# A decoder layer's second FFN: operands on 256-byte lines, weight sums on VectorE, two of eight pairs with seven products

## The chip, the cores and the metric

The kernel runs on one core of one Trainium2 chip. The metric is the device time of one execution in microseconds. A profile is taken of one further execution. In the profile PE is TensorE (its weight loads are listed as PEld), DVE is VectorE, ACT is ScalarE, POOL is GpSimd, and SP is the engine whose queue issues the weight loads from HBM.

## The reference, cut to what matters

One layer of a decoder, for 256 tokens and 16 meta tokens, width 2048, in float32. The change lies in the last step, the second SwiGLU FFN; the first FFN and the attention, convolution and merge ahead of it ("the mix") keep their instructions.

```python
D_MODEL, SEQ, D_FF = 2048, 256, 5632

def swiglu(x, w_gate, w_up, w_down):
    return (jax.nn.silu(x @ w_gate) * (x @ w_up)) @ w_down

h = h + 0.5 * swiglu(rms_norm(h, ffn1_norm_g), ffn1_w_gate, ffn1_w_up, ffn1_w_down)
...
u = rms_norm(h, ffn2_norm_g[l])
h = h + 0.5 * swiglu(u, ffn2_w_gate[l], ffn2_w_up[l], ffn2_w_down[l])
return h[:, N_META:]
```

## The kernel before, in words

**Numbers.** Every float32 operand is split into a high part (`whi`, rounded to the matmul's format) and a low part (`wlo`, what is left). A product of two such operands is three matmuls: high by high, high by low, low by high (`mac3`, lines 1053 to 1055).

**The weight stream.** Class `Stream` brings the weights in the order in which TensorE uses them. A load is 1 MB (128 rows of 2048 floats, tile `raw`), issued on SP's queue (line 130). It is cut into sub-blocks of at most 1024 columns. For each sub-block ScalarE writes `whi` (line 175) and VectorE writes `wlo = raw - whi` (line 176). `next()` hands the next block of weights to TensorE. When a new sub-block begins it first runs what was put off with `early`, then splits the sub-block that lies a fixed number of places ahead, then runs what was put off with `later`. So the program order of ScalarE and VectorE is set by these three calls. In the second FFN there are six pairs of buffers for split sub-blocks, and a sub-block is split five places ahead of TensorE: the split of sub-block n waits until TensorE has read sub-block n - 6.

**The second FFN.** The 5632 hidden columns are 11 groups of 512. An "up" group forms gate and up for all 256 tokens, from 8 pairs of 256 input rows. For each pair the work is a 2 x 2 by 2 x 2 block product (two halves of the tokens and of the input rows, against gate and up weights). A pair of kind `C` takes the eight plain products: 24 matmuls of 512 columns, two sub-blocks of 1024 columns. A pair of kind `S` takes seven products (the Strassen-Winograd form): 21 matmuls, from four sub-blocks: the weight sums `sa` (1024 columns) and `sb` (1024), two raw blocks (1024) and one (512). The sums of the weights are made by GpSimd (`sum` and `sum_rest`, lines 145, 159 and 160), the sums of the tokens by GpSimd as well (`sums_of_tokens`), once for each pair. The products are gathered in the eight PSUM banks `q1` to `q8`; the seven-product terms are put together on VectorE and ScalarE in `after_seven`, `after_gate`, `after_up` and `products`. Four of the eight pairs of every up group are `S`. A "down" step multiplies the gated result (`mid`, transposed by `turn_mid`) of two or three groups by the down weights, in two halves of 1024 output columns, all of it by plain products, and adds to `ht` (line 1215). `PLAN` lists the order: up, up, down and so on, one group behind.

**The start of the second FFN.** `act2` is the input in split form. The first group also transposes `h` into `ht` (`turn_h`, line 1110, after its first two pairs, into the banks `q1`, `q5`, `q6`, `q7`), makes two of the four token sums, and runs `norm2` (lines 1096 and 1100), which gives the scale `r2` that the gate needs.

**Places in SBUF.** Tiles stand in pools one behind the other, and unused `fill` tiles shift what follows. Counted from the sizes of the tiles, the streamed weight tiles of the pool `splitp` begin 192 bytes behind a multiple of 256 bytes, those of `split2` 224 bytes behind, `mid` of the second FFN 224, `more` (token sums) 192, and `act` on a multiple of 256. In the second FFN the weights are the moving operand of the matmul (512 columns) and the tokens the stationary one (128 columns); in the first FFN and most of the mix it is the other way round.

Of the kernel before, what the change touches and what calls it, by code (L numbers as in the profile page):

```python
# [76 lines left out]
class Stream:  # L77
# [7 lines left out]
    def __init__(self, nc, raw_pool, split_pool):  # L85
# [6 lines left out]
        self.seven, self.n_sums = [], 0  # L92
# [31 lines left out]
    def load(self, upto):  # L124
# [8 lines left out]
        self.sum()  # L133

    def sum(self):

        nc = self.nc
        while self.sum_pool and self.n_sums < len(self.seven):
            g = self.seven[self.n_sums]
            if g >= self.n_loaded or len(self.sums) > 1:  # L140
                return
            raw = self.raw[g]
            a21 = raw[:, 3 * WIDE :].rearrange("p (q c) -> p q c", q=1).to_broadcast([P, 2, WIDE])
            sa = self.sum_pool.tile([P, 2 * WIDE], F32, name="sa", bufs=2)
            nc.gpsimd.tensor_add(  # L145
                sa.rearrange("p (q c) -> p q c", q=2),
                raw[:, WIDE : 3 * WIDE].rearrange("p (q c) -> p q c", q=2),
                a21,
            )
            self.sums[g] = [sa, None]  # L150
            self.n_sums += 1
            if len(self.sums) == 1:
                self.sum_rest(g)

    def sum_rest(self, g):

        nc, raw, sa = self.nc, self.raw[g], self.sums[g][0]
        sb = self.sum_pool.tile([P, 2 * WIDE], F32, name="sb", bufs=1)
        nc.gpsimd.tensor_add(sb[:, :WIDE], sa[:, WIDE:], raw[:, WIDE : 2 * WIDE])
        nc.gpsimd.tensor_add(sb[:, WIDE:], sb[:, :WIDE], raw[:, :WIDE])  # L160
        self.sums[g][1] = sb

    def split(self, upto):
        nc = self.nc
        while self.n_split < min(upto, len(self.subs)):
            g, kind, c, kk, width = self.subs[self.n_split]
            self.load(g + self.raw_bufs)
            n = kk * width
            raw = self.raw[g] if kind == "raw" else self.sums[g][kind == "sb"]
            raw = raw[:, c : c + n]  # L170
# [4 lines left out]
            nc.scalar.activation(hi[:, :n], raw, AF.Copy)  # L175
            nc.vector.tensor_sub(lo[:, :n], raw, hi[:, :n].bitcast(F32))  # L176
# [4 lines left out]
            if kind == "sb":  # L181
                del self.sums[g]
                for x in self.sums:
                    self.sum_rest(x)
                self.sum()
# [48 lines left out]
def tile_decoder_layer(  # L234
# [56 lines left out]
    for kind, at in PLAN:  # L291
        for k, _ in pairs_of(at) if kind == "up" else [("C", 0)] * (len(at) * 4):
            st.add_pair(w2[i], k)
            i += 1
# [13 lines left out]
    const.tile([P, 56], F32, name="fill")  # L308
# [236 lines left out]
    with ExitStack() as mix:  # L545
# [4 lines left out]
        R2 = mp.tile([P, T], F32, name="R2")  # L550
# [458 lines left out]

        def sums_of_tokens(i, to, room):  # L1010
# [6 lines left out]
            nc.gpsimd.tensor_sub(t[:, 0, :], x[:, 0, :P], x[:, 0, P:])  # L1017
            nc.gpsimd.tensor_sub(t[:, 1, :], x[:, 0, P:], x[:, 1, P:])
            nc.gpsimd.tensor_add(t[:, 2, :], x[:, 1, P:], t[:, 0, :])
            nc.gpsimd.tensor_sub(t[:, 3, :], x[:, 1, :P], t[:, 2, :])  # L1020
# [5 lines left out]
        for d in range(KD):  # L1026
# [4 lines left out]
            if d in (1, 5):  # L1031
                st.later(lambda d=d: sums_of_tokens(d // 2, spare[:, d // 4], lambda x: soft_tile(x)[:, :WIDE]), 3)
# [11 lines left out]
    r2 = left.tile([P, 2 * NT], F32, name="r2")  # L1044
# [27 lines left out]
    mids, waiting = {}, []  # L1072

    def turn_mid(tags):
# [4 lines left out]
        pool = left if g % 3 == 2 else right[0]  # L1079
        to = pool.tile([P, 4, 2, SEQ], F32R, name="mid", tag=f"mid{g % 3}")  # L1080
        mids[g] = to
        for j in range(NT):
# [4 lines left out]
            def after(j=j, ps=ps):  # L1087
                cols = slice(j * P, (j + 1) * P)
                src = ps.rearrange("p (f t) -> p f t", f=4)
                split_into(to[:, :, 0, cols], to[:, :, 1, cols], src)  # L1090

            st.later(after, 1 + j)

# [19 lines left out]
    def up_group(g):  # L1113
        todo = pairs_of(g)
        kinds = [k for k, _ in todo]
# [246 lines left out]
```

## Time and profile before

| | us |
|---|---|
| median of three runs (2247.4 to 2256.06) | 2249.43 |
| the profiled execution | 2250.48 |
| its span, first to last instruction | 2248.7 |
| second FFN in it, from the last `po` product to the end | about 1450 to 2249 |
| PE busy over the span | 2180.6 |

How to read it: the profiled execution took 1.8 us more than its span and 1.05 us more than the median. A matmul's record ends after the next one has begun, so the time that a run of matmuls takes is read from their starts, not from the mean duration.

### The profile page before, as it was taken

The page shows a single profiled execution, that of the slowest core. Times are in us where ns is not written, and L with a number is a line of the kernel's source. Part 1 is how long each engine was busy: PE and PEld are TensorE (multiplying, and loading weights), DVE is VectorE, ACT ScalarE, POOL GpSimd, SP SyncE. Part 2 cuts the span into 40 slices and gives each one's busy share as a digit, 9 for nine tenths or more (in the row PEclk, how much of TensorE's full clock was granted, in tenths as well). Part 3 has the DMA queues.
Part 4 walks back from the last instruction along what each step waited for, and adds up shares of the span by engine and source line. Part 5 has one row for each costly group of instructions (what it writes and reads, how often), then busy time and mean ns, then how long its engine had stood idle before and what let it go on. Part 6 is the DMA issues. An engine that isn't in the chain of part 4 may idle for free.

```text
span 2248.7 us, 32711 instructions
## 1 busy us (share of the span) xinstructions
PE 2180.6 (97%) x13445; PEld 1957.0 (87%) x13445; DVE 1505.7 (67%) x1762; ACT 1063.1 (47%) x1417; POOL 341.2 (15%) x191
## 2 busy tenths in 40 slices
PE   8999999999999999999999999978999989989899
PEld 8999999999999998889988888866877868778687
DVE  7555544555555555786666776868879788797884
ACT  6434433344434445554444555545545455454552
POOL 3000000000000000000000001255244252542520
PEclk9999999999999999999999999989999999999999
DMA  6555555555555545444555555544645546455453
GB/s 241 186 183 171 172 185 172 184 169 175 182 169 182 175 162 181 141 165 143 189 194 188 187 192 189 190 141 160 215 150 175 195 156 213 161 181 193 150 210 108
DMA packets 56310, 397.75 MB, mean 177 GB/s; under 512 B 6272, under 2 KB 6400, under 8 KB 8672
## 3 DMA queue, kind: packets, MB, share of 16 engines
q1 hardware_dynamic: 55872, 395.08, 50.8%
q8 instruction: 105, 1.72, 0.3%
q0 software_dynamic: 144, 0.42, 0.1%
q14 instruction: 45, 0.37, 0.0%
q10 hardware_dynamic: 144, 0.17, 0.0%
HBM read 393.54 MB, written 2.10 MB: 176 GB/s over the span
## 4 chain that ended last, share of the span: by engine, by line
PE 87%; DVE 8%; ACT 1%; POOL 1%; issue 1%; DMA 0%; SPq 0%; DVEq 0%; ACTq 0%; POOLq 0%
DVE wlo L176 6%; PE pgt L363 5%; PE q L1053 5%; PE q L1055 5%; PE q L1054 5%; PE pd L346 4%; PE pd L347 4%; PE pd L348 4%; PE pg L347 4%; PE pu L347 4%; PE pu L348 4%; PE pg L348 4%; PE pg L346 4%; PE pu L346 4%; PE pd L1053 4%; PE pd L1054 4%
## 5 line engine op out<-in xcount | busy, mean ns | idle before, releaser
L176 DVE TENSOR_TENSOR wlo<-raw,whi 128x1024 fp32r<-128x1024 f32 (+1 forms) x747 | 986.1, 1331 | 645.0 <-ACT whi L175 643.8
L175 ACT ACTIVATE whi<-raw 128x1024 fp32r<-128x1024 f32 (+1 forms) x747 | 765.7, 1032 | 885.1 <-PE pd L347 145.8
L1053 PE MATMUL q<-whi,act 128*128 128x512 f32 x577 | 236.6, 410 | 44.6 <-DVE ve L1149 16.4
L1054 PE MATMUL q<-wlo,act 128*128 128x512 f32 x577 | 233.1, 404 | 1.2 <-DVE wlo L176 1.2
L1055 PE MATMUL q<-whi,act 128*128 128x512 f32 x577 | 233.3, 404 | 0.0
L346 PE MATMUL pd<-mid,whi 128*128 128x272 f32 x704 | 201.7, 287 | 0.0
L348 PE MATMUL pd<-mid,wlo 128*128 128x272 f32 x704 | 201.7, 287 | 0.0
L347 PE MATMUL pd<-mid,whi 128*128 128x272 f32 x704 | 201.7, 286 | 0.0
L346 PE MATMUL pg<-act,whi 128*128 128x272 f32 x672 | 193.4, 288 | 0.0
L348 PE MATMUL pg<-act,wlo 128*128 128x272 f32 x672 | 193.2, 288 | 0.0
L347 PE MATMUL pu<-act,whi 128*128 128x272 f32 x672 | 193.2, 288 | 0.0
L348 PE MATMUL pu<-act,wlo 128*128 128x272 f32 x672 | 193.2, 288 | 0.0
L347 PE MATMUL pg<-act,whi 128*128 128x272 f32 x672 | 193.2, 288 | 0.0
L346 PE MATMUL pu<-act,whi 128*128 128x272 f32 x672 | 193.2, 287 | 0.0
L1053 PEld LDWEIGHTS q<-whi,act 128*128 128x128 f32 x577 | 112.1, 194 | 76.7 <-ACT whi L175 18.4
L145 POOL TENSOR_TENSOR sa<-raw 128x1024 f32<-128x1024 f32 x43 | 118.2, 2748 | 286.4 <-DMA raw<-in_w_dram 286.4
L411 POOL TENSOR_TENSOR ssq<-ssq,sq 128x272 f32<-128x272 f32 (+1 forms) x21 | 22.4, 1065 | 822.1 <-ACT sq L406 821.5
L1053 PE MATMUL pd<-whi,mid 128*128 128x512 f32 x352 | 139.2, 395 | 0.0
L1054 PE MATMUL pd<-wlo,mid 128*128 128x512 f32 x352 | 138.8, 394 | 0.0
L1055 PE MATMUL pd<-whi,mid 128*128 128x512 f32 x352 | 138.5, 393 | 0.0
L1054 PEld LDWEIGHTS q<-wlo,act 128*128 128x128 f32 x577 | 112.3, 195 | 28.2 <-DVE wlo L176 2.0
L1055 PEld LDWEIGHTS q<-whi,act 128*128 128x128 f32 x577 | 111.7, 194 | 27.5
(266 smaller groups left out, 4334.2 us busy)
## 6 DMA issues: line engine op xcount, KB each, us to landing
raw<-in_w_dram SPq DMA_DIRECT2D x132, 1024.0 KB, 4.9
raw<-in_wgu_dram SPq DMA_DIRECT2D x87, 1024.0 KB, 4.8
raw<-in_wd_dram SPq DMA_DIRECT2D x44, 1024.0 KB, 4.9
raw<-in_wcv_dram SPq DMA_DIRECT2D x24, 1024.0 KB, 4.9
raw<-in_wgc_dram SPq DMA_DIRECT2D x24, 1024.0 KB, 4.9
raw<-in_wga_dram SPq DMA_DIRECT2D x24, 1024.0 KB, 4.9
raw<-in_wo_dram SPq DMA_DIRECT2D x16, 1024.0 KB, 4.9
raw<-in_wqi_dram SPq DMA_DIRECT2D x8, 1024.0 KB, 4.9
```

Of the source, the lines that this page charges most:

```text
L145: nc.gpsimd.tensor_add(sa.rearrange("p (q c) -> p q c", q=2), raw[:, WIDE : 3 * WIDE].rearrange("p (q c) -> p q c", q=2), a21,)
L175: nc.scalar.activation(hi[:, :n], raw, AF.Copy)
L176: nc.vector.tensor_sub(lo[:, :n], raw, hi[:, :n].bitcast(F32))
L346: nc.tensor.matmul(ps, whi, xhi, start=first, stop=False)
L347: nc.tensor.matmul(ps, whi, xlo, start=False, stop=False)
L348: nc.tensor.matmul(ps, wlo, xhi, start=False, stop=last)
L363: nc.tensor.matmul(ps.rearrange("p (a t) -> p a t", a=2), whi, x(i), start=i == 0, stop=False)
L411: eng.tensor_add(to, to, sq)
L1053: nc.tensor.matmul(ps, xhi, whi, start=n == 0, stop=False)
L1054: nc.tensor.matmul(ps, xhi, wlo, start=False, stop=False)
L1055: nc.tensor.matmul(ps, xlo, whi, start=False, stop=n == total - 1)
```

## The change

- The kinds of the pairs: two of eight pairs of an up group are `S` (before: four), and the down phase uses the same form: two of the eight pairs of each half, one of six in the last step.
- The plan: up groups 0 to 3, one down step over all four, then 4 to 7, then 8 to 10. `mid` is one tile of four slots in a pool on the right side.
- The weight sums move from GpSimd to VectorE, and are emitted right ahead of the split that needs them (`total`). The sub-blocks of an `S` pair come in the order `one` (512), `sa`, `sb`, `two` (1024, two strided blocks).
- `group` serves both phases. The terms of seven products are put together in `recombine`, put off with `early`; the end of a group (`after_end`) is put off with `early` too, and takes four additions. Gate and up scale and silu follow.
- `turn_h` moves to the last three pairs of the first group, and only two token sums of the input are needed; both are made while the mix ends. For the down phase a token sum is made after `turn_mid` of five groups.
- `r2` moves to the pool `const`, the fill there grows from 56 to 64 floats, `R2` is padded to 320 floats, and the right pool gets 56 floats of fill. Counted from the sizes, `whi`, `wlo`, `mid` and `more` then begin on multiples of 256 bytes. The pools stand one behind the other, so the stationary weights of the first FFN and the mix move from 192 to 0 as well, and the first FFN's `mid` rows from 128 to 192.

```diff
-SEVEN = "SCSCSSCC"
-ORDER = [0, 1, 2, 3, 4, 6, 5, 7]
-FIRST_KINDS = "CCSCSSCC"
-FIRST_ORDER = [1, 3, 0, 5, 2, 4, 6, 7]
...
+KINDS = "SCCSCCCC"
+ORDER = [2, 0, 1, 4, 3, 5, 6, 7]
+PARTS = [range(0, 4), range(4, 8), range(8, NG)]
+PLAN = [step for gs in PARTS for step in [("up", g) for g in gs] + [("down", gs)]]
+
+
+def pairs_up(g):
+    return list(zip("CCSCSCCC", range(PAIRS)) if g == 0 else zip(KINDS, ORDER))
+
+
+def pairs_down(gs):
+    at = [(g, f) for g in gs for f in (0, 2)]
+    return [(k, g, f) for k, (g, f) in zip(KINDS if len(gs) > 3 else "SCCCCC", at)]
...
-            (g, "sa", 0, 2, WIDE), (g, "sb", 0, 2, WIDE), (g, "raw", 0, 2, WIDE), (g, "raw", 2 * WIDE, 1, WIDE)
+            (g, "one", WIDE, 1, WIDE), (g, "sa", 0, 2, WIDE), (g, "sb", 0, 2, WIDE), (g, "two", 0, 2, WIDE)
...
+    def total(self, g, kind):
...
+        if kind == "sa":
+            self.nc.vector.tensor_add(
+                to.rearrange("p (q c) -> p q c", q=2),
                 raw[:, WIDE : 3 * WIDE].rearrange("p (q c) -> p q c", q=2),
-                a21,
+                raw[:, 3 * WIDE :].rearrange("p (q c) -> p q c", q=1).to_broadcast([P, 2, WIDE]),
             )
...
+            self.nc.vector.tensor_add(to[:, :WIDE], sa[:, WIDE:], raw[:, WIDE : 2 * WIDE])
+            self.nc.vector.tensor_add(to[:, WIDE:], to[:, :WIDE], raw[:, :WIDE])
...
-    const.tile([P, 56], F32, name="fill")
+    r2 = const.tile([P, 2 * NT], F32, name="r2")
+    const.tile([P, 64], F32, name="fill")
...
-        R2 = mp.tile([P, T], F32, name="R2")
+        R2 = mp.tile([P, PITCH], F32, name="R2")[:, :T]
...
+        def recombine():
+            a, v, x, e = (small_tile(n) for n in "avxe")
+            buf.update(q2=a, q3=v, q4=x, q8=e)
+            nc.scalar.activation(a, q["q1"][0], AF.Copy)
+            nc.vector.tensor_sub(v, q["q6"][0], a)
+            nc.vector.tensor_add(x, q["q7"][0], v)
+            nc.vector.tensor_sub(v, q["q5"][0], v)
+            nc.vector.scalar_tensor_tensor(e, q["q5"][0], -1.0, x, op0=ALU.mult, op1=ALU.add)
+            after_seven(buf)
...
+                if n == 5:
+                    norm2()
+                if n >= 5:
+                    for i in range(3 * n - 15, min(3 * n - 12, 8)):
+                        turn_h(i // 2, i % 2, ("q7", "q6", "q5")[i % 3])
...
+            for tag in ("q3", "q2", "q4", "q8"):
+                nc.vector.tensor_add(buf[tag], q[tag][0], buf[tag])
...
+            wide_mid = right[0].tile([P, len(PARTS[0]) * 8 * SEQ + 56], F32R, name="mid")
```

**Place 1, the end of an up group on VectorE.** Before, from the two last additions of group 1 (`ve`, `vx` from the banks `q4`, `q8`) to the first splits of group 2:

```order
L1149 TENSOR_TENSOR ve_15546<-q4_15234,vx_15452 128x512
L1150 TENSOR_TENSOR vx_15452<-q8_15260,vx_15452 128x512
L176 TENSOR_TENSOR wlo_15558<-sa_15403,whi_15557 128x1024
L1155 TENSOR_TENSOR vx_15452<-vx_15452,vc_15447 128x512
L1158 SCALAR_TENSOR_TENSOR m0_15562<-ve_15546,r2_14751,va_15449 128x512
L1158 SCALAR_TENSOR_TENSOR m1_15563<-vx_15452,r2_14751,vv_15451 128x512
L176 TENSOR_TENSOR wlo_15575<-sb_15444,whi_15574 128x1024
L176 TENSOR_TENSOR wlo_15592<-raw_15401,whi_15591 128x1024
L176 TENSOR_TENSOR wlo_15599<-raw_15401,whi_15598 128x512
```

Now, at the same place of the program, with the four additions that free `q3`, `q2`, `q4` and `q8`:

```order
L1183 TENSOR_TENSOR vv_15315<-q3_15185,vv_15315 128x512
L1183 TENSOR_TENSOR va_15314<-q2_15189,va_15314 128x512
L1183 TENSOR_TENSOR vx_15316<-q4_15197,vx_15316 128x512
L1183 TENSOR_TENSOR ve_15317<-q8_15219,ve_15317 128x512
L173 TENSOR_TENSOR wlo_15494<-raw_15296,whi_15493 128x1024
L173 TENSOR_TENSOR wlo_15504<-raw_15327,whi_15503 128x1024
L1190 SCALAR_TENSOR_TENSOR vm0_15507<-vx_15316,r2_87,va_15314 128x512
L1190 SCALAR_TENSOR_TENSOR vm1_15508<-ve_15317,r2_87,vv_15315 128x512
```

The additions stand ahead of the new split now, not behind one, and the split behind them is of a plain block.

**Place 2, one seven-product pair on VectorE, now** (`sumsa` and `sumsb` are the weight sums; before, VectorE held only the four splits of lines 176, as at the end of the first piece, and GpSimd the sums):

```order
L173 TENSOR_TENSOR wlo_15534<-raw_15361,whi_15533 128x512
L140 TENSOR_TENSOR sumsa_15544<-raw_15361 128x1024
L173 TENSOR_TENSOR wlo_15547<-sumsa_15544,whi_15546 128x1024
L147 TENSOR_TENSOR sumsb_15563<-sumsa_15544,raw_15361 128x512
L148 TENSOR_TENSOR sumsb_15563<-sumsb_15563,raw_15361 128x512
L173 TENSOR_TENSOR wlo_15567<-sumsb_15563,whi_15566 128x1024
L173 TENSOR_TENSOR wlo_15583<-raw_15361,whi_15582 128x1024
```

Each sum stands right ahead of the split that reads it, with ScalarE's `whi` of the sum between the two.

**Place 3, the first group on TensorE.** Before, the second set of transposes of `h`, then the first product of the first `S` pair:

```order
L1055 MATMUL q8_14795<-whi_14763,act_77 128x512
L1110 MATMUL pht_14880<-ident_85,h_76 128x128 x4
L1110 MATMUL pht_14885<-ident_85,h_76 128x128 x4
L1110 MATMUL pht_14890<-ident_85,h_76 128x128 x4
L1110 MATMUL pht_14895<-ident_85,h_76 128x128 x4
L1053 MATMUL q7_14900<-whi_14769,act_77 128x512
```

Now, in the middle of the sixth pair:

```order
L1054 MATMUL q3_14753<-whi_14905,act_77 128x512
L1118 MATMUL norm_14990<-ones_86,ssq0_78 128x2 x2
L1128 MATMUL pht_14996<-ident_85,h_76 128x128 x4
L1128 MATMUL pht_15001<-ident_85,h_76 128x128 x4
L1128 MATMUL pht_15006<-ident_85,h_76 128x128 x4
L1052 MATMUL q4_14784<-whi_14921,act_77 128x512
```

The transposes have moved behind both `S` pairs of the group, next to the sum of squares for the norm.

More of the change, by code (lines that the diff above doesn't have):

```diff
@@ L181, in split @@
             if kind == "sb":
[L182 to L185, printed above, removed]
+                del self.sums[g, kind]
             if self.n_split == len(self.subs) or self.subs[self.n_split][0] > g:
@@ L291, in tile_decoder_layer @@
     for kind, at in PLAN:
[L292 removed]
+        for k in [p[0] for p in (pairs_up(at) if kind == "up" else pairs_down(at) * 2)]:
             st.add_pair(w2[i], k)
@@ L1070, in plain_half, with small_tile @@
         mac3(c2, b12, w)
-    mids, waiting = {}, []
+    mids, waiting, made_mid = {}, [], {}
+    part = {g: gs for gs in PARTS for g in gs}
+    slot = {g: i for gs in PARTS for i, g in enumerate(gs)}
+    def small_tile(name):
+        return left.tile([P, WIDE], F32, name=f"v{name}", tag=f"v{name}")
     def turn_mid(tags):
@@ L1078, in turn_mid @@
         g, m = waiting.pop(0)
-        pool = left if g % 3 == 2 else right[0]
-        to = pool.tile([P, 4, 2, SEQ], F32R, name="mid", tag=f"mid{g % 3}")
+        to = right[0][:, slot[g]]
         mids[g] = to
+        ks = [f // 2 for k, gg, f in pairs_down(part[g]) if gg == g and k == "S"]
+        if ks:
+            x = small_tile("x2").rearrange("p (i t) -> p i t", i=2)
         for j in range(NT):
@@ L1090, in after, with sums @@
                 split_into(to[:, :, 0, cols], to[:, :, 1, cols], src)
+                if ks:
+                    nc.scalar.activation(x[:, :, cols], src[:, 2 * ks[0] : 2 * ks[0] + 2, :], AF.Copy)
             st.later(after, 1 + j)
+        if ks:
+            def sums():
+                t = small_tile("t4")
+                sums_into(t, x)
+                two = more[:, len(made_mid) % 2]
+                split_into(two[:, 0, :], two[:, 1, :], t)
+                made_mid[g, 2 * ks[0]] = two
+            st.later(sums, 3)
     def norm2():
@@ L1173, in up_group @@
+        for n, (kind, four, ts) in enumerate(todo):
+            b11, b12, b21, b22 = four()
+            if kind == "S":
+                t1, t3, t2, t4 = (both(ts()[:, :, f * P : (f + 1) * P]) for f in range(4))
+                mac3(of("q1"), b11, st.next())
+                for tag, t in (("q7", t3), ("q5", t1), ("q6", t2), ("q3", b22), ("q2", b21), ("q4", t4)):
+                    mac3(of(tag), t, st.next())
                 if "S" not in kinds[n + 1 :]:
-                    st.later(lambda: copies("c", "q5"))
@@ new lines, in tile_decoder_layer, with place, add_half, after_seven @@
+    PLACES = {"q2": (0, 0), "q3": (1, 0), "q4": (0, 1), "q8": (1, 1)}
+    def down_group(gs, final):
+        pairs = pairs_down(gs)
+        for half in range(2):
+            def place(tag, half=half):
+                j, c = PLACES[tag]
+                c = half * 2 * WIDE + c * WIDE
+                return j, c, ht[j][:, c : c + WIDE]
+            def add_half(to, x):
+                nc.vector.scalar_tensor_tensor(to, x, 0.5, to, op0=ALU.mult, op1=ALU.add)
+            def after_seven(buf, place=place):
+                for tag in PLACES:
+                    add_half(place(tag)[2], buf[tag])
+            def after_end(q, buf, place=place):
+                for tag in ("q3", "q2", "q4", "q8"):
+                    j, c, to = place(tag)
+                    add_half(to, q[tag][0])
@@ L1216, in after @@
                     if final:
                         nc.sync.dma_start(out[j * P : (j + 1) * P, c : c + WIDE], to)
-            st.later(after)
+            group(
+                [
+                    (k, lambda g=g, f=f: four_of(mids[g], f, f + 1), lambda g=g, f=f: made_mid[g, f])
+                    for k, g, f in pairs
+                ],
+                lambda n: n == len(pairs) - 4 and half == 0 and turn_mid(("q1", "q5")), after_seven, after_end,
+            )
     right = []
```

186 lines of the change are left out of this document (61 added, 125 removed).

## The prediction, on record before the changed kernel was run

> **What bounds the kernel now.** I read the page's first part, then a table of the stages, then the rows of the stage that the change rewrites.
>
> ```profile
> PE 2180.6 (97%) x13445; PEld 1957.0 (87%) x13445; DVE 1505.7 (67%) x1762; ACT 1063.1 (47%) x1417; POOL 341.2 (15%) x191
> ```
>
> TensorE bounds the kernel as a whole. The busy time by stage (first FFN, mix, first group of the second FFN, the rest of it; the columns are PE, PEld, DVE, ACT, POOL, granted clock, DMA share, GB/s) shows where it doesn't:
>
> ```profile
> 0.00:800.00 800.00, 791.76 (x6323) 790.99 (x6324) 432.25 (x524) 335.53 (x413) 23.75 (x29) 1.00 0.53 181
> 800.00:1450.00 650.00, 648.66 (x3960) 572.61 (x3960) 441.90 (x706) 340.28 (x572) 21.85 (x26) 1.00 0.52 178
> 1450.00:1580.00 130.00, 108.28 (x457) 85.81 (x457) 103.62 (x90) 66.66 (x85) 70.73 (x37) 0.92 0.42 148
> 1580.00:2249.00 669.00, 631.94 (x2711) 507.61 (x2709) 527.92 (x443) 320.60 (x349) 224.86 (x101) 0.98 0.50 176
> ```
>
> ```profile
> 2244.36 0.40 PE L1055 MATMUL pd<-whi,mid 128*128 128x512 f32 x1
> ```
>
> In the second FFN PE idles 21.7 + 37.1 = 58.8 us. About 4.2 of that lies behind its last matmul, which ends at 2244.76, so 54.6 us are waits. The granted clock is 0.92 and 0.98 there and 1.00 before: 8% of 108.3 and 2% of 631.9 is another 21.3 us. Together **76 us are lost** in this stage. Both have one source, as the start of an up group shows on PE, DVE and POOL (start, duration, instruction):
>
> ```profile
> 1659.10 0.40 PE L1055 MATMUL q<-whi,act 128*128 128x512 f32 x1
> 1662.97 0.50 PE L1053 MATMUL q<-whi,act 128*128 128x512 f32 x1 [3.48 <-DVE ht L1215]
> 1663.93 0.63 PE L1053 MATMUL q<-whi,act 128*128 128x512 f32 x1
> 1664.36 0.63 PE L1054 MATMUL q<-wlo,act 128*128 128x512 f32 x1
> 1667.18 0.39 PE L1055 MATMUL q<-whi,act 128*128 128x512 f32 x1
> 1667.41 0.40 PE L1053 MATMUL q<-whi,act 128*128 128x512 f32 x1
> ```
> ```profile
> 1658.52 3.20 DVE L176 TENSOR_TENSOR wlo<-raw,whi 128x1024 fp32r<-128x1024 f32 x1 [1.58 <-ACT whi L175]
> 1661.64 2.47 DVE L1215 SCALAR_TENSOR_TENSOR ht<-pd,ht 128x512 f32<-128x512 f32 x4
> ```
> ```profile
> 1658.27 2.37 POOL L145 TENSOR_TENSOR sa<-raw 128x1024 f32<-128x1024 f32 x1 [5.71 <-DMA raw<-in_w_dram]
> ```
>
> TensorE needs a PSUM bank that VectorE must empty first. The four additions wait behind a split that takes 3.20 us, while GpSimd adds weights beside it. After the wait the matmuls start 0.43 us apart (1663.93, 1664.36) and only 3 us later 0.23 apart (1667.18, 1667.41): that is the lost clock. The split alone is far shorter, as the rows by shape show, first of the first FFN, then of the second, then GpSimd's sums:
>
> ```profile
> L176 DVE TENSOR_TENSOR wlo<-raw,whi 128x1024 fp32r<-128x1024 f32 x265 | 326.0, 1231 | 357.6 <-ACT whi L175 357.6
> ```
> ```profile
> L176 DVE TENSOR_TENSOR wlo<-raw,whi 128x1024 fp32r<-128x1024 f32 x218 | 334.9, 1554 | 108.5 <-ACT whi L175 107.5
> L176 DVE TENSOR_TENSOR wlo<-sa,whi 128x1024 fp32r<-128x1024 f32 x43 | 77.5, 1803 | 13.4 <-ACT whi L175 13.4
> L176 DVE TENSOR_TENSOR wlo<-sb,whi 128x1024 fp32r<-128x1024 f32 x43 | 53.5, 1245 | 10.7 <-ACT whi L175 10.2
> ```
> ```profile
> L145 POOL TENSOR_TENSOR sa<-raw 128x1024 f32<-128x1024 f32 x43 | 118.2, 2748 | 286.4 <-DMA raw<-in_w_dram 286.4
> L159 POOL TENSOR_TENSOR sb<-sa,raw 128x512 f32<-128x512 f32 x43 | 93.8, 2181 | 112.6 <-DVE wlo L176 111.3
> L160 POOL TENSOR_TENSOR sb<-sb,raw 128x512 f32<-128x512 f32 x43 | 80.2, 1864 | 3.4
> ```
>
> A split of 1024 columns takes 1.23 us where GpSimd rests, 1.55 to 1.80 on average where it adds: the two engines hold each other up.
>
> **The change part by part**, against the profiled execution, 2250.5 us (2248.7 of span and 1.8 around it; 1.05 above the median shown).
>
> *Products.* Before: 44 `S` pairs of 21 matmuls and 88 `C` pairs of 24, together 3036. After: up 22 `S` and 66 `C`, down 10 `S` and 34 `C`, together 3072. At 0.229 us (below) the 36 more cost **+8.2 us**. Transposes and the 132 weight loads keep their number.
>
> *The step of a matmul.* Starts of matmuls with 512 moving columns, from a down step, and the chain of waits for the mix, whose moving operand lies on a line already:
>
> ```profile
> 1617.68 0.39 PE L1054 MATMUL pd<-wlo,mid 128*128 128x512 f32 x1
> 1619.49 0.39 PE L1053 MATMUL pd<-whi,mid 128*128 128x512 f32 x1
> ```
> ```profile
> 1612.00:1656.00 44.00, 43.37 (x187) 34.87 (x187) 2.47 (x4) 1.00 0.47 161
> ```
> ```profile
> 1097.50 1.83 PE pgt L363 x8
> ```
>
> Eight steps from 1617.68 to 1619.49 are 0.226 us each, the best I find; the down stretch as a whole has 187 in 43.37 us, 0.232; the mix 1.83 / 8 = 0.229. I take 0.232 before and 0.229 after: 3036 x -0.003 = **-9.1 us**, with the ends 0 and -18 (0.226). The Trainium skill speaks against this part: its page "SBUF — State Buffer", section "Specifications (TRN2)", gives lines of 16 bytes, and 192 and 224 are multiples of 16 already. By that rule the term is 0.
>
> *First FFN and mix.* Only addresses move there. The two address pairs of the first FFN (gate and up: moving 192, stationary 192; down: 128 and 192) step like this:
>
> ```profile
> 100.00:140.00 40.00, 40.00 (x322) 40.00 (x321) 21.18 (x27) 16.48 (x21) 0.00 (x0) 1.00 0.52 182
> 300.00:340.00 40.00, 40.00 (x326) 40.00 (x325) 17.69 (x18) 14.84 (x14) 0.00 (x0) 1.00 0.51 171
> ```
>
> 40 / 322 = 0.1242 against 40 / 326 = 0.1227, 1.5 ns apart. Afterwards both have 192 and 0, which no row shows. If the 2112 down matmuls take gate's step it is +3 us, if the 4032 others take down's it is -6. I take 0.
>
> *The waits.* Without GpSimd's sums every split costs 1.23 us. VectorE gets the sums instead, 32 pairs of them. No row shows them on VectorE; the nearest is the split itself, also two float32 operands in SBUF, so 1.23 for `sumsa`, and for 512 columns the subtraction into `mid`:
>
> ```profile
> L384 DVE TENSOR_TENSOR mid<-pt,mid 128x512 fp32r<-128x512 f32 x22 | 15.0, 683 | 0.0
> L1158 DVE SCALAR_TENSOR_TENSOR m<-ve,r,va 128x512 f32<-128x512 f32 x11 | 8.2, 745 | 0.0
> L1215 DVE SCALAR_TENSOR_TENSOR ht<-pd,ht 128x512 f32<-128x512 f32 x40 | 25.0, 679 | 12.3 <-PE pd L1055 12.3
> ```
> ```profile
> L175 ACT ACTIVATE whi<-raw 128x1024 fp32r<-128x1024 f32 x218 | 228.6, 1059 | 207.1 <-PE pd L1055 100.7 <-PE q L1055 90.2 <-issue 10.7
> L1142 ACT ACTIVATE va<-va,r 128x512 f32<-128x512 f32 x11 | 8.0, 724 | 32.7 <-DVE va L1141 32.7
> ```
>
> 1.23 + 2 x 0.68 = 2.6 us (ends: 2.6, and GpSimd's own 2.75 + 2.18 + 1.86 = 6.8). Each sum also adds a wait: VectorE stands until ScalarE has made `whi` of it, 1.06 us, twice in a pair. So an `S` pair costs VectorE 3 x 1.23 + 0.68 + 2.6 + 2.1 = 9.1 us, a `C` pair 2.5. An up group: 2 x 9.1 + 6 x 2.5 = 33.2, `recombine` 4 x 0.68, the four additions 2.7, the two products 1.5, `mid` 1.4: **41.5 us, against 186 x 0.229 = 42.6 on TensorE** and 0.9 for transposes. A down half: 33.2 + 2.7 + 8 x 0.68 + 0.7 = 42.0. VectorE fits, at 95 and 99%, and has five sub-blocks of lead to even out the two dear pairs.
>
> At the end of a group the additions stand right behind the last split for which buffers were free, ahead of the next one. VectorE reaches them about when the last product ends; `q3` is free 0.7 us after, and the next group wants it only after four products that use `q1`, `q7`, `q5` and `q6`, 12 x 0.23 = 2.75 us. So the wait of 3.48 us goes. Behind the additions stand ScalarE's two silu (0.72 each) and then `whi` of a plain sub-block, which TensorE needs 7.5 us into the group. Late next would be the second `S` pair. VectorE's queue from the group's start: additions 2.7, waiting for silu and `whi` 1.2, two splits 2.5, products 1.5, a split 1.2, `one` 0.7, `sa` with its sum and wait 3.5, `sb` 3.7, together 17.0 us. TensorE wants `sb` after 21 + 48 + 9 matmuls, at 17.9. A lead of 0.9 us is left.
>
> In the first group, the wait for the transposes goes (their banks are free by then), the one for the norm stays:
>
> ```profile
> PEld q L1053 <- ACT ht L1111: 7.8, 1, 7.8
> PE norm L1100 <- DVE ssq L1096: 6.1, 1, 6.1
> ```
>
> `norm` still stands behind VectorE's splits and behind `recombine`. I count 4 us for it and 2 for the slow clock after it, 1 for the change from the mix, and 0.5 for each of the 17 groups: 15 us of waits where 76 were, **-61 us**. The tail keeps its last additions and stores.
>
> Sum: 2250.5 + 8.2 - 9.1 + 0 - 61 = 2188.6, or about **2188** by the median shown. Ends: 2250.5 + 8.2 - 18 - 6 - 66 = 2169 with waits of 10, and 2250.5 + 8.2 + 0 + 3 - 51 = 2211 with waits of 25.
>
> **The rivals.**
> - *VectorE has no lead at the `S` pairs.* A group leaves VectorE 1 or 2 us, and without a lead each pair's wait for ScalarE falls on TensorE: 32 x 1.06 = 34 us, **2222**. For it: GpSimd's token sums make ScalarE wait too, ahead of `whi`. Against it: the six `C` pairs of a group leave 3 us each.
> - *The lines do nothing*, so the change isn't what it says: the step stays at 0.232 and the first FFN's down takes gate's step: +9 + 3, **2200**. For it: the best step, 0.226, belongs to operands that both lie 224 behind a line.
> - *Both operands on a line gain twice.* From 0.232 to 0.226 is what the address pairs of the down rows differ by; as much again, 0.220, gives 3072 x -0.009 = -28, **2160**. No row goes that low. The skill's page "TensorE: Matmul & The Clock Gate", section "Back-to-back issue gap", has 512 / 2.4 + 2.5 = 216 ns, an estimate that lies beyond even this.
> - *Sums on VectorE cost what they did on GpSimd*, 6.8 us (broadcast and strided operands are not in any VectorE row). Then a group takes 41.5 + 2 x 4.2 = 49.9 us on VectorE, which becomes the bound: 15 such groups and two of 34 are 817, with start and tail 831 instead of 799 us, **2282, slower**. It decides from 48 us a group on, that is sums of 5.9 us. Against it: a split is two reads and a write as well, and takes 1.23.
>
> **How the numbers follow.** Forecast 0.60, 2169 to 2211 by itself. No lead 0.16, no effect of lines 0.12, twice the gain 0.04, dear sums 0.08. The range 2166 to 2226 leaves out the last two and little else. About 0.5%, 11 us, is what a measurement of this kernel can tell from no change. Faster by more than that is everything but dear sums and the worst of "no lead" (0.04 within 11 us): faster 0.88, same 0.04, slower 0.08.
>
> **What would show it.** Right: in the second FFN a clock of 1.00 but for the first group, splits of 1.23 us, GpSimd idle but for five token sums, PE idle of 10 to 15 us, steps of 0.229. Wrong: waits of `q` on `wlo` or `whi` behind `sumsa` and `sumsb` (no lead), `sumsa` well over 1.3 us (dear sums), unchanged steps (no lines), or a first FFN that isn't 800 us long. A new wait of the first loads on the tiles of the mix, in whose place `raw2` now stands, would make the first group worse than I count.

## The result, and the profile after

| | before | after |
|---|---|---|
| median, us | 2251.35 (2247.4 to 2256.06, 4 runs) | 2176.93 (2175.91 to 2178.33, 4 runs) |
| span of the profiled execution | 2248.7 | 2174.8 |
| ratio of the times, 95% interval | | 0.9669 (0.9648 to 0.969) |

The changed kernel is 74 us faster. The forecast was 2188, its range 2166 to 2226.

First the page of the changed kernel (engine, busy time, share of the span, instructions), then its stages (busy time of PE, PEld, DVE, ACT and POOL, granted clock, DMA share, GB/s):

```profile
PE 2151.6 (99%) x13478; PEld 1953.8 (90%) x13478; DVE 1448.4 (67%) x1871; ACT 1038.3 (48%) x1399; POOL 56.6 (3%) x74
```
```profile
0.00:800.00 800.00, 791.37 (x6383) 790.68 (x6384) 437.35 (x531) 338.27 (x419) 24.93 (x31) 1.00 0.53 183
800.00:1450.00 650.00, 646.99 (x3909) 571.68 (x3909) 439.00 (x704) 339.97 (x570) 20.61 (x23) 1.00 0.52 178
1450.00:1560.00 110.00, 106.25 (x482) 88.50 (x481) 83.05 (x97) 58.33 (x70) 2.21 (x4) 0.98 0.48 172
1560.00:2175.00 615.00, 606.98 (x2709) 502.92 (x2708) 488.98 (x541) 301.78 (x341) 8.81 (x16) 1.00 0.53 190
```

In the second FFN (the last two rows) PE idles 3.75 + 8.02 us where it idled 58.8, some 4 of them behind the last matmul. The clock is 0.98 in the first group and 1.00 after it; before it was 0.92 and 0.98.

A second count goes by the starts of the matmuls. Where a step is over 0.06 us too long, all that is above the usual step (0.236 us with 512 columns, 0.13 otherwise) counts as lost. It takes idle time and slow clock together: **75.1 us lost before, 15.6 after** in the second FFN. All experiments below are counted in this way.

What is left of waits stands in the waits view of the second FFN (waiting tile and line, releaser: total us, how many, longest us):

```profile
PE pt L1091 <- DVE ve L1151: 3.9, 2, 2.0
PE norm L1118 <- DVE ssq L1114: 3.7, 1, 3.7
...
PE q L1052 <- ACT u L374: 1.8, 1, 1.8
```

No product of a group waits for `wlo` or `whi` behind a sum. The groups of VectorE's splits and sums in the second FFN (last columns: busy us, mean ns, idle time before them):

```profile
L173 DVE TENSOR_TENSOR wlo<-raw,whi 128x1024 fp32r<-128x1024 f32 x229 | 269.1, 1221 | 43.0 <-ACT whi L172 42.8
L173 DVE TENSOR_TENSOR wlo<-sumsb,whi 128x1024 fp32r<-128x1024 f32 x32 | 39.2, 1226 | 38.6 <-ACT whi L172 38.6
L173 DVE TENSOR_TENSOR wlo<-sumsa,whi 128x1024 fp32r<-128x1024 f32 x32 | 39.2, 1225 | 47.3 <-ACT whi L172 47.3
L140 DVE TENSOR_TENSOR sumsa<-raw 128x1024 f32<-128x1024 f32 x32 | 39.1, 1221 | 0.0
L148 DVE TENSOR_TENSOR sumsb<-sumsb,raw 128x512 f32<-128x512 f32 x32 | 23.0, 720 | 1.1
...
L147 DVE TENSOR_TENSOR sumsb<-sumsa,raw 128x512 f32<-128x512 f32 x32 | 21.9, 685 | 0.0
```

A split costs 1.22 us where it averaged 1.55, and the three sums of a pair together 1.221 + 0.685 + 0.720 = 2.63 us. 47.3 / 32 = 1.5 us of idle time stand before each split of `sumsa` and 38.6 / 32 = 1.2 before each of `sumsb`: VectorE waiting for ScalarE.

### The profile page after: what moved, and what is told of

Its sections match the earlier page's. It is cut to its first block, busy times and chain, and to the rows that moved or that the text cites. A ratio compares the mean times of both kernels' runs of the same rounds, so it can differ in the third digit from the quotient of the medians.

```text
span 2174.8 us, 32667 instructions
## 1 busy us (share of the span) xinstructions
PE 2151.6 (99%) x13478; PEld 1953.8 (90%) x13478; DVE 1448.4 (67%) x1871; ACT 1038.3 (48%) x1399; POOL 56.6 (3%) x74
## 4 chain that ended last, share of the span: by engine, by line
PE 94%; DVE 3%; ACT 2%; issue 1%; DMA 0%; POOL 0%; SPq 0%; ACTq 0%; DVEq 0%
PE q L1052 10%; PE q L1053 10%; PE q L1054 10%; PE pgt L358 5%; PE pd L342 4%; PE pd L341 4%; PE pd L343 4%; PE pu L341 4%; PE pu L343 4%; PE pg L343 4%; PE pg L341 4%; PE pg L342 4%; PE pu L342 4%; PE pgt L360 3%; PE pbr L358 3%; PE po L358 2%
## 5 line engine op out<-in xcount | busy, mean ns | idle before, releaser
L173 DVE TENSOR_TENSOR wlo<-raw,whi 128x1024 fp32r<-128x1024 f32 (+1 forms) x747 | 884.3, 1200 | 573.7 <-ACT whi L172 572.6
L1052 PE MATMUL q<-whi,act 128*128 128x512 f32 x682 | 267.7, 392 | 1.8 <-ACT u L374 1.8
L1054 PE MATMUL q<-whi,act 128*128 128x512 f32 x682 | 266.5, 391 | 0.0
L1053 PE MATMUL q<-wlo,act 128*128 128x512 f32 x682 | 266.4, 391 | 0.0
L1052 PEld LDWEIGHTS q<-whi,act 128*128 128x128 f32 x682 | 128.7, 189 | 28.4 <-ACT u L374 2.0
L1054 PEld LDWEIGHTS q<-whi,act 128*128 128x128 f32 x682 | 128.5, 188 | 26.9
L1053 PEld LDWEIGHTS q<-wlo,act 128*128 128x128 f32 x682 | 128.6, 189 | 26.2
L343 PEld LDWEIGHTS pd<-mid,wlo 128*128 128x128 f32 x704 | 132.7, 189 | 0.0
L341 PEld LDWEIGHTS pd<-mid,whi 128*128 128x128 f32 x704 | 132.7, 189 | 0.0
L342 PEld LDWEIGHTS pd<-mid,whi 128*128 128x128 f32 x704 | 132.7, 189 | 0.0
L358 PE MATMUL pgt<-act,whi 128*128 128x512 f32 x512 | 128.2, 393 | 0.0
L342 PEld LDWEIGHTS pg<-act,whi 128*128 128x128 f32 x672 | 126.7, 189 | 0.0
```

Of the source, the lines that this page charges most:

```text
L173: nc.vector.tensor_sub(to[1], raw, to[0].bitcast(F32))
L341: nc.tensor.matmul(ps, whi, xhi, start=first, stop=False)
L342: nc.tensor.matmul(ps, whi, xlo, start=False, stop=False)
L343: nc.tensor.matmul(ps, wlo, xhi, start=False, stop=last)
L358: nc.tensor.matmul(ps.rearrange("p (a t) -> p a t", a=2), whi, x(i), start=i == 0, stop=False)
L1052: nc.tensor.matmul(ps, xhi, whi, start=n == 0, stop=False)
```

## The experiments

Each kernel was timed beside the kernel before on its chip, whose median lay between 2251.7 and 2257.8 us. Mean steps by class of operand are worked out from the starts of the matmuls in the trace; for a step read from a row, the matmuls that overlap the window are counted.

### Do the lines shorten the step?

**The lines taken back** in the changed kernel:

```diff
-    const.tile([P, 64], F32, name="fill")
+    const.tile([P, 48], F32, name="fill")
-        R2 = mp.tile([P, PITCH], F32, name="R2")[:, :T]
+        R2 = mp.tile([P, PITCH + 16], F32, name="R2")[:, :T]
-            wide_mid = right[0].tile([P, len(PARTS[0]) * 8 * SEQ + 56], F32R, name="mid")
+            wide_mid = right[0].tile([P, len(PARTS[0]) * 8 * SEQ + 64], F32R, name="mid")
```

> The changed kernel with its operands put back on the offsets of before (weights of the second FFN at 192 mod 256 bytes, mid at 224; first FFN and mix as before too); nothing else differs. Theory (the lines shorten the step): 512-column steps of the second FFN go back from 0.227 to 0.232 us, 3072 x 0.0053 = +16; gate and up of the first FFN +8, the mix -4.5: about 2197 us. Rival (the steps are shorter because GpSimd is idle or because the order differs): steps stay at 0.227, 2177 us within 4.

Measured: 2199.44 us (2198.56 to 2199.99), ratio 0.9762 (0.9746 to 0.9779). **The lines alone are worth 22 us of the 74.** By class: the second FFN's step goes from 226.8 ns to 233.2, gate and up of the first FFN from 123.3 to 125.3, while the two steps of the mix's `pgt`, `pbr` and `po` fall from 230.1 to 228.9 and from 119.1 to 115.7. That is 3072 x 6.4 + 4032 x 2.0 - 1024 x 4.6 = 19.7 + 8.1 - 4.7 = 23.1 us. The 384 products of the mix that have moving weights (`pi`, `pq`) add 2 more, with steps of 227 to 228 ns that go to 233.3. The waits hardly change (14.2 us lost), and the sum comes out 1 to 2 us above what was measured.

**The lines alone in the kernel before** (`r2` moved to `const`, its fill 64, `R2` padded, 56 floats of fill behind the second `mid`):

> The kernel before with only the lines of the change (weights, act and mid of the second FFN all at 0 mod 256). Theory (lines act by themselves): steps 0.227, 3036 x 0.0053 = -16, first FFN and mix -4: about 2231 us, if the waits stay at 75 us. Rival 1 (lines do nothing): 2251. Rival 2 (the waits end at times that VectorE sets, so that a faster TensorE only waits longer): steps 0.227, but idle time of PE in the second FFN up by about 10 us, and 2240 to 2251.

Measured: 2236.86 us (2235.41 to 2238.96), ratio 0.993 (0.9915 to 0.9945), 16 us less. The same views of its second FFN:

```profile
1450.00:1580.00 130.00, 109.76 (x470) 89.30 (x469) 104.62 (x89) 67.80 (x85) 70.72 (x36) 0.91 0.45 154
1580.00:2238.00 658.00, 618.63 (x2678) 507.01 (x2676) 519.09 (x440) 316.10 (x344) 214.58 (x98) 0.97 0.51 176
```

The step is 0.227 here too, but the clock falls from 0.92 and 0.98 to 0.91 and 0.97, and 84.4 us are lost in place of 75.1. Both readings hold in part: the lines act by themselves, and where VectorE sets the end of a wait, a faster TensorE waits longer.

### Is it a line at all?

The prediction had read the effect as a line of 256 bytes. Two kernels move all of SBUF's operands together, by 128 and by 64 bytes (`lead` is the first tile of `const`; shown for 128):

```diff
-    const.tile([P, 32], F32, name="lead")
+    const.tile([P, 64], F32, name="lead")
-            wide_mid = right[0].tile([P, len(PARTS[0]) * 8 * SEQ + 56], F32R, name="mid")
+            wide_mid = right[0].tile([P, len(PARTS[0]) * 8 * SEQ + 24], F32R, name="mid")
```

> The changed kernel with everything in SBUF moved up by 128 bytes: whi, wlo, act, more and mid of the second FFN all lie at 128 mod 256, so that all offsets between operands stay as they are and only the place on the line changes. One look. Theory A (the place on a 256-byte line decides): steps of 0.232 to 0.234, as with unequal offsets, 2192 to 2198 us. Theory B (only that moving and stationary operands lie alike decides): 0.227, 2177 us. Theory C (lines of 128 bytes): 0.227 here, but not with everything at 64.

> The same with 64 bytes: all operands of the second FFN at 64 mod 256. Theory A: 0.232 to 0.234, 2192 to 2198 us. Theory B: 0.227, 2177 us. Theory C: 0.232 to 0.234 here. The pairs of before that lay alike, 192 with 192 and 224 with 224, took 0.230 and 0.2285, which is between A and B.

A third gives each buffer another offset:

```diff
-            hi = pool.tile([P, SUB], F32R, name="whi")
-            lo = pool.tile([P, SUB], F32R, name="wlo")
+            hi = pool.tile([P, SUB + 8], F32R, name="whi")[:, :SUB]
+            lo = pool.tile([P, SUB + 8], F32R, name="wlo")[:, :SUB]
...
+            wide_mid = right[0].tile([P, 4 * (8 * SEQ + 8) + 24], F32R, name="mid")
...
```

> The changed kernel with 32 bytes of room behind each buffer of whi and wlo and behind each slot of mid, so that the moving operand of the second FFN goes through 0, 32, 64, ... 224 mod 256 bytes and the stationary mid through 0, 32, 64, 96. One look, for the step of a product by offset. Theory A (lines of 256 bytes): 0.227 at 0 alone and 0.233 at the seven others, about 2193 us. Theory B (a shorter line): 128 as good as 0 with lines of 128, 64 and 192 too with lines of 64. Theory C (the moving operand does not matter, the stationary does): one step for all moving offsets.

Measured, one execution each: **2175.21 us at 128, 2177.57 at 64, 2209.15 with mixed offsets**. One stretch of the second FFN without waits or transposes (columns as in the stages above), for the changed kernel, all at 128, all at 64, the lines taken back, and mixed offsets:

```profile
1945.00:2045.00 100.00, 100.00 (x443) 82.85 (x442) 80.00 (x88) 50.85 (x54) 0.00 (x0) 1.00 0.55 197
```
```profile
1945.00:2045.00 100.00, 100.00 (x443) 82.84 (x442) 80.02 (x87) 51.47 (x55) 0.00 (x0) 1.00 0.55 200
```
```profile
1945.00:2045.00 100.00, 100.00 (x443) 82.81 (x442) 79.99 (x86) 50.78 (x54) 0.00 (x0) 1.00 0.55 196
```
```profile
1945.00:2045.00 100.00, 100.00 (x431) 80.61 (x430) 76.15 (x83) 48.37 (x51) 0.00 (x0) 1.00 0.51 180
```
```profile
1945.00:2045.00 100.00, 100.00 (x433) 80.93 (x432) 77.28 (x85) 46.24 (x48) 0.00 (x0) 1.00 0.54 189
```

A matmul's record lasts 0.39 us, and those that overlap an edge count, so the step is 100.39 / n: 0.2266 three times, then 0.2329 and 0.2318. All stages of the kernels at 64 and 128 step as in the changed kernel, to 0.1 ns (226.8, 123.3, 230.1 and 119.1 by class). **So it is not the place on a line, but how the operands lie to each other.** Theory B holds for these two, A and C fall. A still shorter line falls as well: with the lines taken back, the weights lie at 192 and the stationary `act` at 0, both multiples of 64, and their products step 233.4 ns.

The kernel with mixed offsets says the same from the other side. Mean step of its up products, whose stationary operand lies at 0 throughout, by offset of the moving one:

| 0 | 32 | 64 | 96 | 128 | 160 | 192 | 224 |
|---|---|---|---|---|---|---|---|
| 230.2 ns | 232.5 | 231.2 | 233.6 | 232.8 | 233.5 | 230.5 | 231.0 |

Even products with both operands at 0 take 230.2 ns here and 226.8 in the changed kernel. What differs is the operands of the matmuls around them, and how far apart the buffers lie beyond 256 bytes; no run separates the two. So no single product can be called "on" or "off" the line by its own offset. The first FFN takes part too, with 126.0 ns against 123.3: 6336 x 2.7 = 17 us, which is what 2209 lies above the 2193 expected.

The last kernel of this kind starts from the version without the three waits (further below, 2166.61 us) and moves two other moving operands:

```diff
-            next_act(d, gains[0], 0, LATER)
+            next_act(d, gains[0], 0, 16)
...
-    ffn(0, LATER, done1, 10)
+    ffn(0, 16, done1, 10)
...
-            i_hi, i_lo = (mid[:, :, i, PITCH - n :] for i in range(2))
+            i_hi, i_lo = (mid[:, :, i, 16 : 16 + n] for i in range(2))
...
-        R2 = mp.tile([P, PITCH], F32, name="R2")[:, :T]
+        R2 = mp.tile([P, PITCH + 16], F32, name="R2")[:, :T]
```

> The kernel with the three waits taken away, and with the moving operand 64 bytes ahead of the stationary one (mod 256) in two more places: act and mid of the first FFN (192 bytes ahead until now), and ys, cs and ms of the mix (level until now). Theory (only the distance between moving and stationary operand counts, and in products whose stationary operand is a weight 64 ahead is the best of those seen: 228.9 and 115.7 ns in the mix before, against 230.1 and 119.1 level): 494 pairs of products of the mix 4.6 ns shorter, -2.3 us; in the first FFN 123.3 becomes 120 to 122 ns, 6336 products, -8 to -20: 2145 to 2157 us. Rival (in the first FFN any distance but 192 costs what level did, 125.3): +13 - 2, 2177 us. Rival 2 (the place of one operand counts, not the distance): the mix stays at 230.1 and 119.1.

Measured: 2187.47 us (2186.19 to 2188.36), ratio 0.9698 (0.9685 to 0.9712). A miss: 21 us slower than its base (18 by the two ratios), not faster. 200 us of the first FFN, for before, the changed kernel, and this one:

```profile
300.00:500.00 200.00, 200.00 (x1612) 200.00 (x1611) 97.83 (x110) 75.62 (x81) 0.00 (x0) 1.00 0.52 176
```
```profile
300.00:500.00 200.00, 200.00 (x1624) 200.00 (x1623) 98.08 (x111) 76.86 (x83) 0.00 (x0) 1.00 0.52 179
```
```profile
300.00:500.00 200.00, 200.00 (x1581) 200.00 (x1580) 94.78 (x106) 74.10 (x79) 0.00 (x0) 1.00 0.51 174
```

With moving minus stationary offset at 192 the first FFN steps 123.3 ns, level 125.3, at 64 126.7; 6336 x 3.4 = 21.5 us is the whole loss. In the mix `ms` at 64 gave the 229.0 and 115.8 ns that were hoped for, but `ys` and `cs`, at the same 64, 233.6 and 117.9. The distance mod 256 is therefore not the whole rule either. The changed kernel's own trace shows it too: its `pgt` products with 512 columns come in rows of eight, all with both operands at 0, and by their place in the row they step about 233, 236, 229, 232, 231, 227, 226 and 227 ns, within 2 ns each time.

### The sums

**The sums back on GpSimd**, all else as changed (three `nc.vector.tensor_add` in `total` become `nc.gpsimd.tensor_add`):

> The changed kernel with the 96 weight sums on GpSimd in place of VectorE. Theory (VectorE and GpSimd hold each other up): sums of 2.7, 2.2 and 1.9 us, splits of raw 1.4 to 1.6 us on average in the second FFN where they are 1.22, groups with two S pairs no longer ahead of TensorE, waits of 10 to 35 us more: 2187 to 2212 us. Rival (taking 2.6 us a pair off VectorE outweighs it): splits below 1.3 us, 2177 us or less.

Measured: 2185.02 us (2183.34 to 2186.42), ratio 0.9699 (0.9684 to 0.9713), 8 us more. VectorE's splits and one of GpSimd's sums:

```profile
L173 DVE TENSOR_TENSOR wlo<-raw,whi 128x1024 fp32r<-128x1024 f32 x229 | 336.4, 1508 | 83.3 <-ACT whi L172 83.3
```
```profile
L140 POOL TENSOR_TENSOR sumsa<-raw 128x1024 f32<-128x1024 f32 x31 | 76.8, 2479 | 429.4 <-DMA raw<-in_w_dram 382.7 <-DVE wlo L173 33.8 <-DVE rs_y L418 12.9
```

The split is back at 1.51 us, and 25.3 us are lost, 9.7 more. The contention is real, as the prediction took it, but at two of eight pairs it is the smaller part: putting it back returns 10 us of the 60 by which the waits shrank. One by one, the 162 of these 229 splits that no GpSimd operation overlaps take 1.22 us on average, the 67 others 2.21. By the Trainium skill ("SBUF — State Buffer", section "SBUF: two separate sides") a VectorE operation with two inputs in SBUF, as a split is, and a GpSimd operation that reads SBUF take a shared pair of ports by an exclusive lock, held for the whole instruction; the two averages agree.

### The place of the additions

**Recombine and the end of a group behind the next split:**

```diff
-                    st.early(recombine)
+                    st.later(recombine)
...
-        st.early(lambda: after_end(q, buf))
+        st.later(lambda: after_end(q, buf))
```

> The changed kernel with recombine and the additions at the end of a group put behind the next split on VectorE, as before, in place of ahead of it. Theory (the place of the additions takes the wait for the banks away): they stand behind one split and its whi, 1.2 to 3.5 us, and q3 is free 0.7 later, against 2.75 us of cover by q1, q7, q5 and q6: 0.5 to 1.5 us of wait and as much slow clock in most of 17 groups, 2185 to 2205 us. Rival (the order of the products, an S pair with four other banks first, covers the additions by itself): 2177 us within 4, no new waits of q3.

Measured: 2191.59 us (2190.9 to 2191.92), ratio 0.9728 (0.9713 to 0.9742). 30.3 us are lost, 14.7 more, which is the whole difference. The start of a group on PE and on DVE, first in the changed kernel, where the group begins at 1847.15 and wants `q3` at 1849.87, long after the addition:

```profile
1847.15 0.39 PE L1052 MATMUL q<-whi,act 128*128 128x512 f32 x1
```
```profile
1846.91 0.68 DVE L1183 TENSOR_TENSOR vv<-q,vv 128x512 f32<-128x512 f32 x1
```

Then with the additions behind the split; the group begins at 1851.76 and wants `q3` after the first of these rows:

```profile
1854.25 0.39 PE L1054 MATMUL q<-whi,act 128*128 128x512 f32 x1
1854.99 0.50 PE L1052 MATMUL q<-whi,act 128*128 128x512 f32 x1 [0.35 <-DVE vv L1183]
```
```profile
1853.11 1.23 DVE L173 TENSOR_TENSOR wlo<-raw,whi 128x1024 fp32r<-128x1024 f32 x1 [1.50 <-ACT whi L172]
1854.25 0.68 DVE L1183 TENSOR_TENSOR vv<-q,vv 128x512 f32<-128x512 f32 x1
```

The addition that empties `q3` starts behind a split and its 1.50 us for `whi`, and TensorE, done with `q1`, `q7`, `q5` and `q6`, comes 0.5 us too early. The order of the products hides most of it, not all. So it is at 15 of the 17 group starts, some 9 us with the slow step behind each wait; most of the rest lies at the first transposes of the two longer down steps, which wait about 4 us for `recombine` in place of 2.

### How many pairs VectorE can carry

**Three of eight, and one of eight,** in the up groups (`pairs_up` takes a string of its own, `SCSCSCCC` or `SCCCCCCC`):

> The changed kernel with three in place of two S pairs in each up group but the first (SCSCSCCC; the third takes the token sums of another pair, so this part of the output is not the reference's). Theory (VectorE fits only just at two of eight): a third S pair costs VectorE 9.1 - 2.5 = 6.6 us, 48.1 us a group against 183 x 0.227 + 0.9 = 42.4 on TensorE, so TensorE waits up to 5.7 us in each of 10 groups, less what the sub-blocks of lead even out: 2205 to 2240 us. Rival (VectorE is not near its limit, and the number of S pairs sets only the products): 30 products fewer, 2170 us.

> The changed kernel with one in place of two S pairs in each up group but the first. Theory (two of eight fit beside TensorE at no price): 30 products more at 0.227, +6.8, waits as they are: 2184 us. Rival (the S pairs still cost TensorE waits, at the edge of VectorE's time): waits go with the pair, 2177 us or less.

Measured: three of eight 2237.87 us (2234.97 to 2238.21), ratio 0.9934 (0.9918 to 0.9951); one of eight 2182.45 us (2180.26 to 2183.2), ratio 0.9686 (0.9672 to 0.97). Both as the theory had it: in this order of VectorE's work, two of eight is where TensorE's and VectorE's time meet. With three, 79.3 us are lost; the waits of its second FFN, and VectorE's splits of the sums:

```profile
PE pt L1092 <- DVE ve L1152: 30.4, 10, 3.5
PE q L1054 <- DVE wlo L174: 12.3, 17, 0.8
```
```profile
L174 DVE TENSOR_TENSOR wlo<-sumsb,whi 128x1024 fp32r<-128x1024 f32 x42 | 51.5, 1226 | 50.6 <-ACT whi L173 50.6
L174 DVE TENSOR_TENSOR wlo<-sumsa,whi 128x1024 fp32r<-128x1024 f32 x42 | 51.5, 1226 | 66.2 <-ACT whi L173 66.2
```

VectorE is late with the splits and with `recombine`, whose last step frees the bank of the transposes. Yet it stands idle 50.6 + 66.2 = 117 us in front of these splits, each time for ScalarE's `whi` of a sum that it has only just finished. Hence the next kernel, **three of eight with both sums made ahead of the split of `one`** (and without the three waits below):

```diff
+            if kind == "one":
+                self.total(g, "sa")
+                self.total(g, "sb")
             if kind in ("sa", "sb"):
-                raw = self.total(g, kind)
+                raw = self.sums.pop((g, kind))
```

> Three S pairs in each up group but the first, as before in this study (the third takes the token sums of another pair, so this part of the output is not the reference's), with the three waits taken away, and with both sums of a pair made ahead of its split of one, so that ScalarE makes whi of sumsa and sumsb while VectorE still adds. Theory (a good part of VectorE's price of an S pair is its standing for ScalarE): 9.1 - 2.1 = 7.0 us a pair, 3 x 7.0 + 5 x 2.5 + 8.3 = 41.8 us a group against 42.4 on TensorE, so that the third pair fits: 2166.6 - 30 x 0.227 = 2160 us, at most 5 more. Rival (VectorE's work itself is too much, or the burst of sums uses up the lead of the sub-blocks): 2190 us or more.

Measured: 2165.59 us (2165.28 to 2165.7), ratio 0.9597 (0.9579 to 0.9615).

```profile
L177 DVE TENSOR_TENSOR wlo<-sumsb,whi 128x1024 fp32r<-128x1024 f32 x42 | 52.5, 1249 | 10.9 <-ACT whi L176 10.9
L177 DVE TENSOR_TENSOR wlo<-sumsa,whi 128x1024 fp32r<-128x1024 f32 x42 | 51.2, 1218 | 9.7 <-ACT whi L176 9.7
```

The idle time before the splits of the sums falls from 117 to 21 us, and the third pair fits, though without slack: five waits of `q` for a `wlo` and four for `q3` are left, 8.5 us together. (The token sums that the third pair would need are made in neither of the two kernels with three, so what they cost is not in these times.) It takes 72 us less than three of eight in the plain order, 10 of which the three waits would explain. Against two of eight without the three waits (2166.61) it saves 30 products, 6.8 us, and loses 11.9 - 6.9 = 5.0 us more in waits; the intervals of the two overlap.

### The waits that were left

**Three waits taken away:**

```diff
-                turn_mid(("q1", "q5"))
+                turn_mid(("q1", "q6"))
...
+                if n == 1:
+                    st.later(lambda: nc.vector.tensor_add(ssq[0][:, META:], ssq[0][:, META:], ssq[1][:, META:]))
...
+    for tag in ("q1", "q7", "q5", "q6"):
+        bank(tag, tag)
     right = []
```

(The same bank in the down step, and `norm2` loses its addition.)

> The changed kernel with the three waits that are left taken away at their cause: the transposes take the bank q6, which recombine empties first, in place of q5, which it empties last; the sum of ssq is made on VectorE early in group 0, not behind the splits ahead of norm; q2, q3, q4 and q8 lie on the PSUM banks that the mix leaves free. Theory (each wait is a place in a queue or a bank, and nothing else is late there): of 3.9 at the change from the mix, 5.5 at norm and 5.6 at the two transposes, 10 to 14 us go: 2163 to 2167 us. Rival (behind each the next operation is late, since VectorE is full): less than 5 us go, 2172 us or more.

Measured: **2166.61 us (2165.46 to 2167.31), ratio 0.9617 (0.9602 to 0.9631)**, faster than both kernels of the study. 6.9 us are lost in place of 15.6. Where the second `norm` stood behind VectorE's splits, its timeline now shows:

```profile
1474.03 0.39 PE L1054 MATMUL q<-whi,act 128*128 128x512 f32 x1
1474.25 0.50 PE L1117 MATMUL norm<-ones,ssq 128*128 128x2 f32 x4
1477.04 1.13 PE L1127 MATMUL pht<-ident,h 128*128 128x128 f32 x8 [2.29 <-DVE vx L1148]
```

`norm` follows at once, and what is late next is the transposes of `h`, 2.29 us, for a bank that `recombine` empties. That is why 10 us came and not 14.

## Why the prediction was right, and where it wasn't

- **The waits: 76 to 15 us forecast, 75.1 to 15.6 measured.** The sum is right, the parts are not all. `norm` was taken at 4 + 2 and costs 3.9 + 1.5. The change from the mix was taken at 1 and costs 3.6 with the slow clock behind it. The 17 groups were taken at 0.5 us each; most lose nothing, and what they don't lose went into a wait that the prediction did not name: twice the first transposes of a down step take a bank that `recombine` frees last:

```profile
1652.98 0.60 PE L1091 MATMUL pt<-ident,vm 128*128 128x128 f32 x4
1655.53 0.96 PE L1091 MATMUL pt<-ident,vm 128*128 128x128 f32 x4 [1.95 <-DVE ve L1151]
```

- **VectorE's price of an `S` pair, 9.1 us, and of a group, 41.5 us:** the sums were taken at 2.6 us and cost 2.63, but the two waits for ScalarE, at 1.06 each, cost 1.5 and 1.2. That makes a pair 0.6 us dearer than counted, and a group 42.7 us; against TensorE's 186 x 0.2268 + 0.9 = 43.1 it still fits. The test is three of eight, counted at 48.1 us a group, 49.9 with the dearer waits. There the transposes of two neighbouring up groups, which wait for VectorE, begin 50.0 us apart on average (47.4 to 51.7 over the five such pairs in the trace; 48.8 in the rows shown):

```profile
1580.63 0.60 PE L1092 MATMUL pt<-ident,vm 128*128 128x128 f32 x4
```
```profile
1629.47 0.60 PE L1092 MATMUL pt<-ident,vm 128*128 128x128 f32 x4
```

- **The step: this term was mis-sized, and its reason fell.** Forecast 0.232 to 0.229, -9.1 us; measured 0.2323 to 0.2268 on average, 3072 x 0.0055 = -16.9 us. The failed step is the sentence that the mix's moving operand "lies on a line already", so that its 0.229 shows the step to come. The mix went to 0.230 when its stationary operand moved to the same offset, and operands at 64 or 128 step like those at 0. That the gain lay inside the ends 0 and -18 was luck of a wide bound, not of the reasoning.
- **The rule of 16-byte lines** (the Trainium skill, "SBUF — State Buffer", "Specifications (TRN2)") gave 0 for the term. The trace disagrees with that sum (226.8 against 233.2 ns, all offsets multiples of 16), though the kernels at 64 and 128 show that no line of 256 bytes is at work either. The estimate of 216 ns, worked out from the Trainium skill's page "TensorE: Matmul & The Clock Gate", section "Back-to-back issue gap", is reached nowhere in the changed kernel's second FFN, whose mean is 226.8 and whose shortest step is 224. That section of the Trainium skill gives the formula for matmuls taken singly, and about 131 ns for a stream of them with 512 columns; no step here comes near that either.
- **First FFN and mix, taken as 0:** gate and up -8.1, `pgt`, `pbr` and `po` +4.7, `pi` and `pq` -2.2. With all else the second FFN begins 5.0 us sooner (its last `po` product starts at 1445.03 in place of 1450.07), inside the ends of -6 and +3. Gate and up gained 2.0 ns, more than the 1.5 read from the rows.
- **The products, +8.2:** 36 x 0.227, borne out by one of eight (30 more products, 6.8 us by count, 5.5 measured).
- **The additions ahead of the next split** remove the wait, as said; the price of their old place in the new order is 14.7 us.

In sum, on the spans: -59.5 waits, -16.9 step, +8.2 products, -5.0 first FFN and mix are -73.2 of -73.9 us. The forecast for the profiled execution was 2188.6 and it took 2176.6: of these 12 us, 7.8 are the step and 5.0 the first FFN and mix, less 1.5 us of waits. The waits have more than one cause: sums back on GpSimd return 9.7 us, additions behind the split 14.7, a third `S` pair 63.7. These overlap and can't be added, and the new order of the products and the moved transposes were not tried by themselves. The rival "the lines do nothing", at 2200, is what the kernel without them measured, 2199.4; the mechanism was wrong, its price right. "No lead at the `S` pairs" did not occur at two of eight (no row has a product waiting behind a sum), and in part does at three, with 12.3 us of waits of `q` for a `wlo`. "Dear sums" fell with 2.63 us.

## What to carry to other kernels

Count the time of the engine that prepares operands, group by group, against TensorE's: counted at 41.5 us against 42.6 the waits went, at 48.1 most of the saving was given back. Look at what that engine waits for inside its own work before taking work away from it: making the sums ahead of the first split took 96 us of idle time from in front of the splits that read them. And when addresses move a matmul's step, shift everything together once before calling it alignment.

## What was not expected of the hardware

- In this kernel a matmul's step goes with how the operands lie to each other in SBUF. In the second FFN, with 512 columns, it is 226.8 ns on average with all at one offset (0, 64 or 128 mod 256), 233.2 with the lines taken back and 231.9 with mixed offsets.
- The best relation is not the same everywhere. In the second FFN (tokens stationary, weights moving) level operands are the best seen; in the first FFN (weights stationary) 192 bytes apart beats level by 2.0 ns and 64 loses 1.4; in the mix `ms` and `ys`, equal in distance and shape, differ by 4.6 ns. Level is no guarantee: the level `pgt` products step 226 to 236 ns by their place in the row. What rule gives these was not found. Distances beyond 256 bytes were not varied by themselves, and for the first FFN three distances only were tried.
